# A two-layer hybrid decoder trunk: the memory's keys scaled for both token tiles together, and two pieces of side work moved by units

## The chip, the cores and the metric

The kernel runs on one core of one Trainium2 chip. The time is the device time of an execution in microseconds; the time of a kernel is the median of its runs. Three runs of the kernel before gave 929.42 us in the median, from 928.89 to 930.27.

## The reference

Two layers, sequence of 256, width 1024, batch 1, all in float32. Each layer normalises x and multiplies it with one combined matrix `w_in`, whose columns feed four branches and their gates:

```python
h = rmsnorm(x, norm_mix[l])
z = h @ w_in[l]
z_gm, z_lru, q_s, k_s, v_s, q_x, z_gate = jnp.split(z, IN_SPLITS, axis=-1)
mem_n = rmsnorm(mem, norm_mem[l])
o = [gmlp(z_gm), rglru(z_lru), swa(q_s, k_s, v_s), cross(q_x, mem_n)]
x = x + jnp.sum(sigmoid(z_gate + b_gate) * (o @ w_branch), axis=2) @ w_out[l]
x = x + jnp.square(jax.nn.relu(rmsnorm(x) @ w_ff1[l])) @ w_ff2[l]
```

Two branches matter here. Cross attention has 4 heads of 128 and looks at 256 tokens of a memory: `k, v = split(mem_n @ w_kv)`, keys and queries normalised per head, softmax over the 256 tokens. The RG-LRU branch convolves over 4 positions, then multiplies the result with two block-diagonal matrices, whose sigmoids are its gates, and runs a linear recurrence.

## The kernel before, in words

Tokens lie in two tiles of 128 ("token tile 0 and 1"). Weights come in chunks of 128x1024 floats, called units. For each unit, SP's queue loads the raw chunk (L178), ACT copies it to a rounded format (`wh`, L201) and DVE subtracts that from the raw values (`wl`, L202). `prep` (L182) does this some units ahead, as far as raw tiles (4) and weight tiles (5 pairs) come free. TensorE then multiplies with `wh` and `wl` (all through L255), so that a product in full precision is three matmuls. A unit of a 512-column projection is 12 matmuls of 512 columns.

Results land in PSUM, in two pools of four banks: `ps_mm` (tiles `mm`) for the projections, `ps_ac` (tiles `ac`) for transposes, attention and gates. At the start of a layer TensorE computes, in this order: the memory's keys (units 0 to 3, two `mm` banks, one for each token tile of the memory), the memory's values (units 4 to 7, the other two), the input of the RG-LRU branch (`proj_cols`, L413, units 8 to 11; in the first layer its first half goes to `ac` banks and its second half, units 10 and 11, to `mm` banks), cross attention's queries (12 to 15), the window attention's queries (16 to 19), its keys and values (20 and 21), the gMLP (22 to 29), the RG-LRU's second input (30 to 33), and the branch gates.

What isn't a projection is written as generators in a list, `side`. After each unit (after each two in `proj_cols`), `tick` tops up the weights and calls `next` once on each generator. A bare `yield` therefore means "not before the next unit". An instruction that goes through `late` (L362) is, in the first layer, pinned behind everything traced before it on its engine, which is how a yield sets its earliest place on TensorE. `after(ins, ref)` (L354) pins one instruction behind another one in the order of the same engine, without a wait. Within these pins a planner orders each engine's instructions by simulated times, and the engines then run their queues in that order.

`mem_k_side` (L442) takes the keys' two `mm` banks. For each token tile m it sums squares per head on ACT (`head_sq`, L426 and L431: four squares, each with the read of an accumulator), forms a mean on DVE (L449) and the power -1/2 on POOL (L377), multiplies it with the memory's own norm `rmem` on DVE (L452), and scales the four heads on ACT into SBUF (L455). Only this last step frees the `mm` bank. `rmem` and `rmem2` come from `mem_norm` (L1156 to L1163). `st["scaled", m]` names the last scaling of tile m; the split of unit 11 is pinned behind that of tile 0, the splits of units 12 to 14 and the evacuation of the values (L473) behind that of tile 1. Behind eight yields the keys are transposed (L466).

`xa_side` (L523) copies the queries (L530), sums squares, and one unit later transposes them (L542, L543); another unit later it starts `xa_tok` (L552) for token tile 0 and two units behind that for tile 1. Each computes its scores in two `ac` banks, a softmax (exponentials at L501), transposes of the probabilities (L518, L520) and products with the values.

`lru_side` (L716) convolves on DVE (L727, L730), waits some units, and then computes the gates (two matmuls with `wbd` for each of two column blocks, sigmoids at L740 and L741).

Of the kernel before, what the change touches and what calls it, by code (L numbers as in the profile page):

```python
# [13 lines left out]
AF = mybir.ActivationFunctionType  # L14
ALU = mybir.AluOpType
AX = mybir.AxisListType

P = 128
# [6 lines left out]
EPS = 1e-6  # L25
# [16 lines left out]
def trunk(ctx, tc, x_d, mem_d, memT_d, pc_d, pr_d, bg_d, cs_d, wsT_d, wr_d, wi_d,  # L42
          w_in, w_mem_kv, w_branch, w_out, w_ff1, w_ff2, out_d):
    nc = tc.nc
    act, dve, pool, pe = nc.scalar, nc.vector, nc.gpsimd, nc.tensor
# [23 lines left out]
    def T(pl, shape, dt, tag):  # L69
        cnt[0] += 1  # L70
        return pl.tile(shape, dt, tag=tag, name=f"{tag}_{cnt[0]}")
# [4 lines left out]
    def tq():  # L76
        return T(tqp, [P, 512], F32, "tq")

    def a4():
        return T(a4p, [P, 4, S], F32, "a4")  # L80
# [7 lines left out]
    def pac():  # L88
        return T(ps_ac, [P, 512], F32, "ac")

    def small(n):
        return T(sm, [P, n], F32, f"s{n}")
# [161 lines left out]
    def mm(out, lhsT, rhs, start, stop):  # L254
        return pe.matmul(out, lhsT=lhsT, rhs=rhs, start=start, stop=stop, skip_group_check=True)  # L255
# [18 lines left out]
    def join(out, ps, ref=None):  # L274

        after(act.activation(out=out, in_=ps[:, 1, :], func=AF.Copy), ref)
        dve.tensor_tensor(out=out, in0=ps[:, 0, :], in1=out, op=ALU.add)
# [8 lines left out]
    rmem = T(const, [P, 2], F32, "rmem")  # L286
    rmem2 = T(const, [P, 2], F32, "rmem2")
# [61 lines left out]
    def rsqrt_small(ss, n, inv):  # L349
        ms = small(n)  # L350
        dve.tensor_scalar(out=ms, in0=ss, scalar1=inv, scalar2=EPS, op0=ALU.mult, op1=ALU.add)
        return pow_half(ms, n)

    def after(ins, ref):  # L354

        if ref is not None:
            tc.add_manual_dep(ins.ins, ref.ins.name,
                              mybir.DependencyInfo(mybir.DependencyClass.NoSync, mybir.DependencyReason.DATA),
                              reason="after")
        return ins  # L360

    def late(l, ins):  # L362

        return tc.keep_in_program_order(ins) if l == 0 else ins
# [10 lines left out]
    def pow_half(ms, n):  # L375
        r = small(n)
        pool.tensor_tensor(out=r, in0=ms, in1=mhalf[:, 0:n], op=ALU.pow)  # L377
        return r
# [44 lines left out]

    st = {}

    def head_sq(src, nh, hd, ref):  # L426

        ss = small(nh)
        for h in range(nh):
            junk = tq()[:, 0:hd]  # L430
            after(act.activation(out=junk, in_=src[:, h * hd:(h + 1) * hd], func=AF.Square, accum_out=ss[:, h:h + 1]),  # L431
                  ref)
        return ss
# [8 lines left out]
    def mem_k_side(l, kT, ps):  # L442
        while st["hs"] in side:
            yield
        ks = []
        for m in range(2):
            ss = head_sq(ps[m], 4, P, st["square"] if l or m else st["split", 7])
            ms = small(4)
            dve.tensor_scalar(out=ms, in0=ss, scalar1=rmem2[:, m:m + 1], scalar2=EPS, op0=ALU.mult, op1=ALU.add)  # L449
            r = pow_half(ms, 4)  # L450
            rk = small(4)
            dve.tensor_scalar(out=rk, in0=r, scalar1=rmem[:, m:m + 1], scalar2=0.0, op0=ALU.mult, op1=ALU.add)  # L452
            k = tq()
            for h in range(4):
                st["scaled", m] = act.activation(out=k[:, h * P:(h + 1) * P], in_=ps[m][:, h * P:(h + 1) * P],  # L455
                                                 func=AF.Copy, scale=rk[:, h:h + 1])
            ks.append(k)
        yield
        while st["hs"] in side:
            yield  # L460
        for _ in range(6 if l else 8):
            yield
        for m in range(2):
            pst = pac().rearrange("p (h t) -> p h t", t=P)
            for h in range(4):
                late(l, pe.transpose(pst[:, h, :], ks[m][:, h * P:(h + 1) * P], ident))  # L466
            act.activation(out=kT[:, :, m * P:(m + 1) * P], in_=pst, func=AF.Copy,
                           scale=pc[l][:, C_XK:C_XK + 1])
# [54 lines left out]
    def xa_side(l, ps):  # L523

        oh, ol = st["o"][3]
        qT = a4()
        qs, rs = [], []
        for t in range(2):
            q = tq()
            act.activation(out=q, in_=ps[t], func=AF.Copy)  # L530
            qs.append(q)
        for t in range(2):
            ss = head_sq(ps[t], 4, P, None)
            r = rsqrt_small(ss, 4, 1.0 / P)
            rsc = T(odd, [P, 4], F32, f"xrs{t}")
            dve.tensor_scalar(out=rsc, in0=r, scalar1=P ** -0.5, scalar2=0.0, op0=ALU.mult, op1=ALU.add)
            rs.append(rsc)
        yield
        for t in range(2):
            pst = pac().rearrange("p (h t) -> p h t", t=P)  # L540
            for h in range(4):
                pe.transpose(pst[:, h, :], qs[t][:, h * P:(h + 1) * P], ident)  # L542
            act.activation(out=qT[:, :, t * P:(t + 1) * P], in_=pst, func=AF.Copy,  # L543
                           scale=pc[l][:, C_XQ:C_XQ + 1])
        yield
        kT = st["kTx"]
        for t in range(2):
            side.append(xa_tok(l, t, qT, kT, rs[t], oh, ol))
            yield
            yield  # L550
# [162 lines left out]
    def l2():  # L713
        return T(l2p, [P, 2, S], F32, "l2")

    def lru_side(l, ps, c0):  # L716


        pcl = pc[l]
        xc, r, ig, sq = l2(), l2(), l2(), l2()  # L720
        for j in range(2):
            c = c0 + j
            xb = T(t1p, [P, S + 4], F32, "t1")
            pool.memset(xb[:, 0:3], 0.0)
            join(xb[:, 3:S + 3], ps[j], None if l else st["values"])
            w = [pcl[:, C_CW + 4 * k + c:C_CW + 4 * k + c + 1] for k in range(4)]
            dve.tensor_scalar(out=xc[:, j, :], in0=xb[:, 0:S], scalar1=w[0], scalar2=pcl[:, C_CB + c:C_CB + c + 1],  # L727
                              op0=ALU.mult, op1=ALU.add)
            for k in range(1, 4):
                dve.scalar_tensor_tensor(out=xc[:, j, :], in0=xb[:, k:k + S], scalar=w[k], in1=xc[:, j, :],  # L730
                                         op0=ALU.mult, op1=ALU.add)
        for _ in range((3 if c0 == 0 else 1) + (0 if l else 3)):

            yield
        for j in range(2):
            c = c0 + j
            pg = pac().rearrange("p (a s) -> p a s", a=2)
            for i in range(2):
                late(l, mm(pg[:, i, :], wbd[i][:, c, :], xc[:, j, :], True, True))
            act.activation(out=r[:, j, :], in_=pg[:, 0, :], func=AF.Sigmoid, bias=pcl[:, C_BR + c:C_BR + c + 1])  # L740
            st["sigmoid"] = act.activation(out=ig[:, j, :], in_=pg[:, 1, :], func=AF.Sigmoid,  # L741
                                           bias=pcl[:, C_BI + c:C_BI + c + 1])
        dve.tensor_tensor(out=ig, in0=ig, in1=xc, op=ALU.mult)
        yield
        for j in range(2):
            c = c0 + j
            after(act.activation(out=xc[:, j, :], in_=r[:, j, :], func=AF.Exp, scale=nsp8[l][:, c:c + 1]),
                  st["sigmoid"])
            act.activation(out=r[:, j, :], in_=r[:, j, :], func=AF.Tanh, scale=nsp4[l][:, c:c + 1])
        yield  # L750
        while "sqrt" not in st:
            yield
        tc.keep_in_program_order(act.activation(out=sq, in_=r, func=AF.Sqrt, scale=-1.0))
        dve.scalar_tensor_tensor(out=r, in0=xc, scalar=1.0, in1=r, op0=ALU.add, op1=ALU.mult)
        dve.tensor_scalar(out=r, in0=r, scalar1=1.0, scalar2=0.0, op0=ALU.add, op1=ALU.add)
        dve.scalar_tensor_tensor(out=sq, in0=xc, scalar=1.0, in1=sq, op0=ALU.add, op1=ALU.mult)
        dve.tensor_tensor(out=ig, in0=ig, in1=sq, op=ALU.mult)
        for j in range(2):
            dve.tensor_tensor_scan(out=xc[:, j, :], data0=r[:, j, :], data1=ig[:, j, :], initial=0.0,
                                   op0=ALU.mult, op1=ALU.add)  # L760
        yield
        while "gb" not in st:
            yield
        oh, ol = st["o"][1]
        for j in range(2):
            c = c0 + j
            o = t1()
            dve.tensor_tensor(out=o, in0=xc[:, j, :], in1=st["gb"][:, c, :], op=ALU.mult)
            split(o, oh[:, c, :], ol[:, c, :])
# [397 lines left out]
    for l in range(DEPTH):  # L1167
        st["h"] = new_h()
        h, lo = halves(st["h"])
# [58 lines left out]
```

## Time and profile before

| | |
|---|---|
| median of three runs | 929.42 us |
| profiled execution | 930.37 us |
| its span, first to last instruction | 928.6 us |
| TensorE busy (matmuls) | 922.4 us, 99% |
| VectorE (DVE) busy | 642.2 us, 69% |
| ScalarE (ACT) busy | 545.5 us, 59% |
| GpSimd (POOL) busy | 47.5 us, 5% |
| bytes moved by DMA | 173.56 MB, 187 GB/s in the mean |

Busy times are unions of an engine's instructions. Matmuls overlap each other in the record, so a row's duration is a little longer than the distance to the next row's start. "Idle before" is the time an engine had nothing running ahead of an instruction, with the instruction that released it. The granted clock is a share of TensorE's full 2.4 GHz.

### The profile page before, as it was taken

Reading aid. Unit: us, or ns where it says so; the run is one execution under the profiler, and the core shown is the slowest. Engines: PE = TensorE matmul, PEld = TensorE weight load, DVE = VectorE, ACT = ScalarE, POOL = GpSimd, SP = SyncE. Lnnn points to the kernel's source line nnn. Section 1 sums busy time; section 2 is a strip of 40 time slices with the busy share of each in tenths; the row PEclk is TensorE's granted clock in tenths of the full one; section 3 lists DMA queues with packets and bytes.
Section 4 is the critical chain, followed back from the end, with each engine's and each line's share of the span. In section 5 each row is a group of like instructions: output and inputs, shape, how many; then the busy total and the mean of one; then the engine's idle time right before and its main releaser. Section 6 shows DMA issues by size and latency. Waiting matters only on the chain.

```text
span 928.6 us, 12959 instructions
## 1 busy us (share of the span) xinstructions
PE 922.4 (99%) x4712; PEld 777.4 (84%) x4712; DVE 642.2 (69%) x1055; ACT 545.5 (59%) x913; POOL 47.5 (5%) x93
## 2 busy tenths in 40 slices
PE   9999999999999999999999999999999999999998
PEld 6788887888889888888888888888888898888887
DVE  6686878656686766776577587865666767666663
ACT  7778898444444744645376788874444455544541
POOL 1114300000000000000010230000000000000000
PEclk9999999999999999999999999999999999999999
DMA  9683445666565776776456444466665657666641
GB/s 342 193 253 113 140 153 178 201 216 209 188 196 148 234 228 184 231 234 187 149 163 197 147 133 153 142 185 213 203 213 177 195 175 233 199 190 195 199 141 46
DMA packets 143920, 173.56 MB, mean 187 GB/s; under 512 B 8176, under 2 KB 92656, under 8 KB 143856
## 3 DMA queue, kind: packets, MB, share of 16 engines
q1 hardware_dynamic: 143424, 172.31, 59.9%
q8 instruction: 37, 0.61, 0.3%
q10 hardware_dynamic: 432, 0.43, 0.2%
q14 instruction: 27, 0.22, 0.1%
HBM read 171.66 MB, written 1.05 MB: 186 GB/s over the span
## 4 chain that ended last, share of the span: by engine, by line
PE 95%; DMA 1%; ACT 1%; DVE 1%; issue 1%; POOL 0%; SPq 0%; ACTq 0%
PE mm L255 65%; PE ac L255 28%; DMA raw<-in_w_mem_kv 1%; PE ac L518 1%; DVE wl L202 0%; ACT wh L201 0%; PE mm L801 0%; PE mm L972 0%; POOL s L377 0%; ACT hx L806 0%; PE ac L709 0%; ACT tq L455 0%; ACT tq L431 0%; PE ac L801 0%; PE ac L466 0%
## 5 line engine op out<-in xcount | busy, mean ns | idle before, releaser
L202 DVE TENSOR_TENSOR wl<-raw,wh 128x1024 fp32r<-128x1024 f32 (+1 forms) x276 | 332.3, 1209 | 176.3 <-ACT wh L201 175.9
L201 ACT ACTIVATE wh<-raw 128x1024 fp32r<-128x1024 f32 (+1 forms) x276 | 287.6, 1048 | 254.0 <-PE mm L255 137.3
L255 PE MATMUL mm<-wh,hx 128*128 128x512 f32 (+1 forms) x832 | 257.5, 387 | 0.0
L255 PEld LDWEIGHTS mm<-wh,hx 128*128 128x128 f32 x832 | 153.4, 188 | 29.8 <-issue 0.8
L255 PE MATMUL mm<-wl,hx 128*128 128x512 f32 (+1 forms) x416 | 160.1, 385 | 0.0
L255 PE MATMUL mm<-hx,wh 128*128 128x512 f32 (+1 forms) x496 | 122.4, 381 | 1.8 <-ACT tq L455 1.8
L255 PE MATMUL ac<-wh,s 128*128 128x512 f32 x380 | 121.5, 390 | 0.0
L255 PEld LDWEIGHTS mm<-hx,wh 128*128 128x128 f32 x496 | 89.9, 190 | 17.5 <-ACT tq L455 2.0
L255 PEld LDWEIGHTS mm<-wl,hx 128*128 128x128 f32 x416 | 78.3, 188 | 15.0 <-issue 0.3
L255 PEld LDWEIGHTS ac<-wh,s 128*128 128x128 f32 x380 | 71.4, 188 | 14.4
L255 PE MATMUL ac<-wl,s 128*128 128x512 f32 x190 | 74.2, 390 | 0.0
L255 PE MATMUL mm<-hx,wl 128*128 128x256 f32 x464 | 69.9, 283 | 0.0
L255 PEld LDWEIGHTS mm<-hx,wl 128*128 128x128 f32 x464 | 65.5, 191 | 4.7 <-issue 0.3
L202 DVE TENSOR_TENSOR a<-raw,a 128x1024 fp32r<-128x1024 f32 x32 | 39.2, 1225 | 27.4 <-ACT a L201 27.4
L201 ACT ACTIVATE a<-raw 128x1024 fp32r<-128x1024 f32 x32 | 33.9, 1059 | 38.7 <-PE ac L255 21.5
L255 PE MATMUL mm<-wl,o0h 128*128 128x512 f32 x128 | 50.3, 393 | 0.0
L255 PE MATMUL mm<-wh,o0l 128*128 128x512 f32 x128 | 49.8, 389 | 0.0
L255 PE MATMUL mm<-wh,o0h 128*128 128x512 f32 x128 | 48.7, 395 | 0.0
L255 PE MATMUL mm<-hx,a 128*128 128x512 f32 (+1 forms) x256 | 46.4, 336 | 0.0
L255 PE MATMUL ac<-a,s 128*128 128x512 f32 x192 | 45.7, 390 | 0.0
L255 PEld LDWEIGHTS mm<-hx,a 128*128 128x128 f32 x256 | 40.7, 189 | 5.8
L255 PEld LDWEIGHTS ac<-a,s 128*128 128x128 f32 x192 | 35.5, 188 | 7.1
(214 smaller groups left out, 1146.5 us busy)
## 6 DMA issues: line engine op xcount, KB each, us to landing
raw<-in_w_ff SPq DMA_DIRECT2D x128, 512.0 KB, 4.3
raw<-in_w_in SPq DMA_DIRECT2D x116, 512.0 KB, 4.0
raw<-in_w_branch SPq DMA_DIRECT2D x32, 512.0 KB, 3.6
raw<-in_w_out SPq DMA_DIRECT2D x16, 512.0 KB, 3.6
raw<-in_w_mem_kv SPq DMA_DIRECT2D x12, 512.0 KB, 3.5
bg<-in_bg SPq DMA_DIRECT2D x16, 256.0 KB, 4.0
raw<-in_w_mem_kv SPq DMA_DIRECT2D x8, 256.0 KB, 5.6
xt<-in_x SPq DMA_DIRECT2D x2, 512.0 KB, 6.5
```

Of the source, the lines that this page charges most:

```text
L201: a1 = act.activation(out=wh[:, sl, :], in_=v[:, sl, :], func=AF.Copy)
L202: a2 = dve.tensor_tensor(out=wl[:, sl, :], in0=v[:, sl, :], in1=wh[:, sl, :].bitcast(F32), op=ALU.subtract)
L255: return pe.matmul(out, lhsT=lhsT, rhs=rhs, start=start, stop=stop, skip_group_check=True)
L518: late(l, pe.transpose(ps[:, h, :], Pt[:, h, kt * P:(kt + 1) * P], ident))
```

## The change

In the first layer, `mem_k_side` treats both token tiles in one pass: the squares of both go into one small tile of 8 columns, two means, one power over 8 columns, two factors, and then the eight scalings. The squares of tile 1 are pinned behind the last split of h (`st["turned"][0]`) in place of the memory's own squares. In the second layer the loop still runs tile by tile. `xa_side` yields four times instead of once ahead of the scores in the first layer, and `lru_side` four times instead of three (beside its 3 or 1) ahead of the gates.

```diff
-    def head_sq(src, nh, hd, ref):
-        ss = small(nh)
+    def head_sq(src, nh, hd, ref=None, ss=None):
+        ss = small(nh) if ss is None else ss
...
-        for m in range(2):
-            ss = head_sq(ps[m], 4, P, st["square"] if l or m else st["split", 7])
-            ms = small(4)
-            dve.tensor_scalar(out=ms, in0=ss, scalar1=rmem2[:, m:m + 1], ...)
-            r = pow_half(ms, 4)
-            rk = small(4)
-            dve.tensor_scalar(out=rk, in0=r, scalar1=rmem[:, m:m + 1], ...)
-            k = tq()
-            for h in range(4):
-                st["scaled", m] = act.activation(out=k[:, h * P:(h + 1) * P], ...)
-            ks.append(k)
+        for ms_ in ((0,), (1,)) if l else ((0, 1),):
+            n = 4 * len(ms_)
+            ss, ms, rk = small(n), small(n), small(n)
+            for i, m in enumerate(ms_):
+                head_sq(ps[m], 4, P, st["square"] if l else st["turned"][0] if m else st["split", 7],
+                        ss[:, 4 * i:4 * i + 4])
+            for i, m in enumerate(ms_):
+                h4 = slice(4 * i, 4 * i + 4)
+                dve.tensor_scalar(out=ms[:, h4], in0=ss[:, h4], scalar1=rmem2[:, m:m + 1], ...)
+            r = pow_half(ms, n)
+            for i, m in enumerate(ms_):
+                h4 = slice(4 * i, 4 * i + 4)
+                dve.tensor_scalar(out=rk[:, h4], in0=r[:, h4], scalar1=rmem[:, m:m + 1], ...)
+            for i, m in enumerate(ms_):
+                k = tq()
+                for h in range(4):
+                    st["scaled", m] = act.activation(out=k[:, h * P:(h + 1) * P], ...)
+                ks.append(k)
...
-        yield
+        for _ in range(1 if l else 4):
+            yield
         kT = st["kTx"]
...
-        for _ in range((3 if c0 == 0 else 1) + (0 if l else 3)):
+        for _ in range((3 if c0 == 0 else 1) + (0 if l else 4)):
```

## Rows read from the trace of the kernel before

**Rows 1.** The page: busy time of TensorE, and the costliest group of ACT
```profile
PE 922.4 (99%) x4712; PEld 777.4 (84%) x4712; DVE 642.2 (69%) x1055; ACT 545.5 (59%) x913; POOL 47.5 (5%) x93
...
L201 ACT ACTIVATE wh<-raw 128x1024 fp32r<-128x1024 f32 (+1 forms) x276 | 287.6, 1048 | 254.0 <-PE mm L255 137.3
```
**Rows 2.** Waits of TensorE: line, waited for, us in total, times, longest
```profile
PE mm L255 <- ACT tq L455: 1.8, 1, 1.8
PE ac L255 <- DVE t L1121: 1.3, 1, 1.3
```
**Rows 3.** Busy time by stretch, behind the wait; clock, DMA share, GB/s last
```profile
40.80:44.50 3.70, 3.70 (x10) 2.95 (x11) 1.63 (x2) 3.70 (x7) 0.00 (x0) 0.54 0.15 35
44.50:47.00 2.50, 2.50 (x16) 2.20 (x15) 2.50 (x5) 2.28 (x4) 0.00 (x0) 1.00 0.69 209
```
**Rows 4.** Timeline of TensorE, 36 to 46: start, us, what, idle before
```profile
36.02 2.00 PE L255 MATMUL mm<-hx,wh 128*128 128x512 f32 x8
37.86 1.11 PE L255 MATMUL mm<-hx,wl 128*128 128x256 f32 x8
40.79 3.56 PE L255 MATMUL mm<-hx,wh 128*128 128x512 f32 x8 [1.82 <-ACT tq L455]
...
45.26 0.63 PE L255 MATMUL mm<-wh,hx 128*128 128x512 f32 x2
```
**Rows 5.** Chain of work that ended last, 20 to 60: start, us, what
```profile
21.42 1.03 ACT tq L431 x8
```
**Rows 6.** Timeline of DVE, ACT and POOL, 29 to 43, and the power of 8
```profile
29.62 0.15 DVE L1163 SCALAR_TENSOR_TENSOR rmem<-s 128x2 f32<-128x2 f32 x1
31.20 1.94 POOL L377 TENSOR_TENSOR s<-s,mhalf 128x4 f32<-128x4 f32 x1 [1.54 <-DVE s L449]
33.81 1.15 ACT L455 ACTIVATE tq<-mm,s 128x128 f32<-128x128 f32 x4 [1.23 <-DVE t L332]
35.58 1.10 ACT L201 ACTIVATE wh<-raw 128x1024 fp32r<-128x1024 f32 x1
38.23 1.01 POOL L377 TENSOR_TENSOR s<-s,mhalf 128x4 f32<-128x4 f32 x1 [5.09 <-DVE t L339]
39.59 1.15 ACT L455 ACTIVATE tq<-mm,s 128x128 f32<-128x128 f32 x4 [2.66 <-DVE t L341]
40.61 1.28 ACT L473 ACTIVATE a<-mm,rmem 128x512 f32<-128x512 f32 x2
41.75 2.04 ACT L201 ACTIVATE wh<-raw 128x1024 fp32r<-128x1024 f32 x2
42.87 1.23 DVE L202 TENSOR_TENSOR wl<-raw,wh 128x1024 fp32r<-128x1024 f32 x1 [2.91 <-ACT wh L201]
...
79.16 1.65 POOL L377 TENSOR_TENSOR s<-s,mhalf 128x8 f32<-128x8 f32 x1 [0.62 <-DVE s L351]
```
**Rows 7.** Timeline, 60 to 179: convolution, gates, scores, softmax, products, branch projections
```profile
60.60 0.48 DVE L730 SCALAR_TENSOR_TENSOR l<-t,pc,l 128x256 f32<-128x256 f32 x1
64.32 1.28 ACT L740 ACT_TABLE_LOAD   x1
64.34 1.89 PE L255 MATMUL ac<-l,wbd 128*128 128x256 f32 x8
65.61 0.47 ACT L740 ACTIVATE l<-ac,pc 128x256 f32<-128x256 f32 x1
73.74 1.25 ACT L543 ACTIVATE a<-ac,pc 128x512 f32<-128x512 f32 x2
75.47 3.62 PE L255 MATMUL ac<-a,a 128*128 128x256 f32 x16
89.43 0.57 ACT L501 ACTIVATE s<-ac,s,xrs 128x256 f32<-128x256 f32 x1
101.05 1.09 ACT L520 ACTIVATE pt<-ac 128x512 f32<-128x512 f32 x2
102.68 1.95 PE L255 MATMUL ac<-pt,a 128*128 128x128 f32 x16
178.26 0.39 PE L255 MATMUL mm<-wh,o1h 128*128 128x512 f32 x1
```

More of the change, by code (lines that the diff above doesn't have):

```diff
@@ L445, in mem_k_side @@
         ks = []
-        for m in range(2):
-            ss = head_sq(ps[m], 4, P, st["square"] if l or m else st["split", 7])
-            ms = small(4)
-            dve.tensor_scalar(out=ms, in0=ss, scalar1=rmem2[:, m:m + 1], scalar2=EPS, op0=ALU.mult, op1=ALU.add)
-            r = pow_half(ms, 4)
-            rk = small(4)
-            dve.tensor_scalar(out=rk, in0=r, scalar1=rmem[:, m:m + 1], scalar2=0.0, op0=ALU.mult, op1=ALU.add)
-            k = tq()
-            for h in range(4):
-                st["scaled", m] = act.activation(out=k[:, h * P:(h + 1) * P], in_=ps[m][:, h * P:(h + 1) * P],
-                                                 func=AF.Copy, scale=rk[:, h:h + 1])
-            ks.append(k)
+        for ms_ in ((0,), (1,)) if l else ((0, 1),):
[6 more added lines that the diff above has]
+                h4 = slice(4 * i, 4 * i + 4)
+                dve.tensor_scalar(out=ms[:, h4], in0=ss[:, h4], scalar1=rmem2[:, m:m + 1], scalar2=EPS,
+                                  op0=ALU.mult, op1=ALU.add)
+            r = pow_half(ms, n)
+            for i, m in enumerate(ms_):
+                h4 = slice(4 * i, 4 * i + 4)
+                dve.tensor_scalar(out=rk[:, h4], in0=r[:, h4], scalar1=rmem[:, m:m + 1], scalar2=0.0,
+                                  op0=ALU.mult, op1=ALU.add)
+            for i, m in enumerate(ms_):
+                k = tq()
+                for h in range(4):
+                    st["scaled", m] = act.activation(out=k[:, h * P:(h + 1) * P], in_=ps[m][:, h * P:(h + 1) * P],
+                                                     func=AF.Copy, scale=rk[:, 4 * i + h:4 * i + h + 1])
+                ks.append(k)
         yield
@@ L532, in xa_side @@
         for t in range(2):
-            ss = head_sq(ps[t], 4, P, None)
+            ss = head_sq(ps[t], 4, P)
             r = rsqrt_small(ss, 4, 1.0 / P)
```

## The prediction

> **What bounds the kernel now.** I read the page's first part, the list of waits for TensorE, the stretches around its one long wait, and then the timeline of the other engines back from it. TensorE is busy for 922.4 of 928.6 us [rows 1], so a change of this kind can only take away what TensorE waits, or add to it. The waits name one place inside the layers: 1.8 us, once, for ACT's scaling of the memory's keys at L455 [rows 2]. The clock falls behind it: in the 3.70 us that follow, the granted clock is 0.54 in the mean, and 1.00 again in the next stretch [rows 3]. The matmuls say the same: eight of 512 columns take 2.00 us ahead of the wait and 3.56 us behind it [rows 4]; that is the lower of the two levels, 1.2 instead of 2.4 GHz. So the place costs 1.82 + 3.70 x (1 - 0.54) = 1.82 + 1.70 = 3.52 us.
>
> Why it waits is seen one step back. The second half of the convolution's projection takes two banks of `ps_mm`. The first comes free with the scaling of token tile 0, the second with that of tile 1. Tile 0 is through at 33.81 + 1.15 = 34.96 [rows 6], before TensorE asks at 36.02 [rows 4]. Tile 1 starts its squares only behind tile 0's scaling, and its mean, power and factor follow: power at 38.23, scaling from 39.59 to 40.74 [rows 6]. TensorE could have gone on at 40.79 - 1.82 = 38.97.
>
> **The keys in one go.** ACT: the four squares of tile 1 (with their reads eight instructions; those of tile 0 took 1.03 us [rows 5]) move from behind tile 0's scaling to anywhere behind the last split of h. Nothing is added there. DVE: two means and two factors remain. POOL: two powers of 4 columns (1.94 and 1.01 us) become one of 8. The trace has that form later, at 1.65 us. The first power of 4 was 0.93 us dearer than the second, so I bound the new one by 1.65 and 1.65 + 0.93 = 2.58 us, and take 1.65, the row of its own form [rows 6].
>
> The chain's times: the means can follow rmem2, through at 29.62 + 0.15 = 29.77; before, the power began at 31.20. ACT idles for 1.23 us ahead of 33.81, so the squares find room; if they stand in front instead, the power begins 1.03 us later. So it begins between 31.2 and 32.2, and ends at 32.9 (or 34.8). One factor and the handover took 33.81 - (31.20 + 1.94) = 0.67 us, so I put 0.9 for two: 33.8 (or 35.7). Four scalings take 1.15 us, eight 2.3. Tile 0 is through at 34.9 (or 36.8), tile 1 at 36.1 (or 38.0). If the split of weights for TensorE's next unit (1.10 us at 35.58, pinned behind tile 0's scaling) is put between the two, tile 1 is at 39.1 in the worst case. Needed: 36.02 and 38.97. What is left of the wait lies between nothing and 0.8 us; I take 0.1, from the near end of both. It can't fall below nothing, as TensorE waits nowhere else near it. At the other end, if the order on ACT undoes the edit, all 3.52 us stay.
>
> **What is late next.** With 3.4 us off, the next unit (cross attention's queries, 45.26 before) starts at about 41.9. Its two banks come free with the evacuation of the values (1.28 us, behind the scaling), so at 37.4 to 40.4. Its weights need a split on ACT and a difference on DVE. Before, the difference began 42.87 - 40.74 = 2.1 us behind the scaling and took 1.2. Behind a scaling that ends at 36.1 to 38.0, with 1.1 us for the unit before it, it is through at 40.5 to 42.4; it is wanted two matmuls behind the unit's start, at 42.3. Covered, with nothing to spare at the worse end. The raw tiles' transfers follow these differences in SP's queue, so they come earlier too; the DMA engines are busy for a share of 0.15 behind the wait [rows 3], so there is room. Farther on the splits run ahead: of the 254.0 us that ACT idles in front of them, 137.3 are waits for TensorE to give tiles back [rows 1].
>
> **Gates one unit later.** The gates' matmuls keep their number and size. Before, the convolution's last step ends at 60.60 + 0.48 = 61.08 and the gates start at 64.34 [rows 7]: 3.3 us to spare, and TensorE now comes 3.4 us earlier. Of 512 columns, eight matmuls start within 37.86 - 36.02 = 1.84 us, so a unit of 12 is 2.8 us, and the pin one unit later keeps 3.3 - 3.4 + 2.8 = 2.7 us even if DVE were no earlier. Cost: nothing. Without this edit it would be 0.1 us at most.
>
> **Scores three units later.** The queries' transposed copy ends at 73.74 + 1.25 = 74.99 and the scores begin at 75.47 [rows 7]: 0.5 us to spare. 3.4 us earlier, TensorE would stand here for up to 2.9 us. Three units are 8.3 us, which leaves 8.3 + 0.5 - 3.4 = 5.4 us to spare. Both tokens' scores ran as one block of 16; now the second is pinned two units behind the first, and softmax, transposes and products with the values go along. The result is wanted when TensorE turns to the branch projections at 178.26 [rows 7], 70 us and more behind. Cost: nothing. In exchange the softmax moves in among square roots and GELUs on ACT. A load of an activation table took 1.28 us, and the activation behind it began 0.01 us later (64.32 to 65.61 [rows 7]). Two more (there and back) would be 2.6 us of ACT.
> The Trainium skill ("ScalarE: Activation LUTs", What ACT_TABLE_LOAD costs) puts a switch at about 2.66 us, drain included, so by it those two would be 5.3 us; the row shows no drain behind the load, and the row decides. The same page (Table sets: the hidden batching unit) advises to finish one set's functions before the next, which speaks against this move.
>
> **Sum.** 930.37 us is the profiled execution (span 928.6 and 1.8 around it). 930.37 - 3.52 + 0.1 = 926.95. It ran 0.95 above the median of 929.42, so for the median: 929.42 - 3.42 = 926.0 us. Layer 1 keeps its numbers and its order of work, as both loops have the old form there.
>
> **Rivals.**
> *Given back farther on.* The products with the values start 0.5 us after the copy they need (101.05 + 1.09 = 102.14 against 102.68 [rows 7]). If at such a place ACT and DVE, which carry the same work as before, don't move along, TensorE waits 3.4 - 0.5 = 2.9 us and a gain of 0.5 stays: 928.9. With half of it given back: 927.5. Two more table loads in that chain would do it as well. For it: the slack is that small. Against: the place at 38.97 held up ACT too (2.66 us idle before 39.59 [rows 6]), so ACT and DVE start earlier as well, and cross attention leaves this stretch.
> *It doesn't do what it says.* The order on ACT (split, evacuation or squares ahead of tile 1's scaling) keeps tile 1 well beyond 38.97 and the clock falls again: 929.4. Against: even the worst bound above is 39.1.
> *Slower.* The scores hold two of four `ps_ac` banks per token until their exponentials have read them. Before, the second token's were held from 75.47 + 3.62 = 79.09 to 89.43 + 0.57 = 90.00 [rows 7], 10.9 us. Three units later that hold stands where the window attention's transposes ask for banks. If TensorE stands for half of it, 5.5 us, and loses the clock for 1.70 us once more, the sum is 929.42 - 3.42 + 7.2 = 933.2. It decides from 3.4 + 1.9 = 5.3 us of new waits on. Against: before, both tokens held all four banks at once, and no wait of TensorE on one is listed [rows 2].
>
> **How the numbers follow.** Forecast 0.68; given back 0.17, half of that in part and half in whole; not done 0.06; slower 0.09. A measurement of this kernel tells about 0.2% from no change, which is 1.9 us. Faster by more: 0.68 + 0.08 = 0.76. Within: 0.08 + 0.06 = 0.14. Slower: 0.10 with rounding. The low end is all 3.52 us off and the 0.8 us by which the runs before lie apart around their median, 925.1. The high end takes in the gain given back and some of the runs' spread, 929.1; the slower case and most of the undone one lie outside.
>
> **What would show it.** Right: no wait of TensorE at L455, a granted clock of 1.00 from 20 us on, one power of 8 columns near 31 to 35 us, tile 1 scaled by 38, the queries' projection starting near 42, and everything behind it 3.4 us earlier. Wrong: a wait of TensorE on an `ac` bank or a copy between 70 and 110 us, a second stretch at the lower clock, or table loads in a softmax with TensorE waiting behind it.

## The result: 934.33 us, slower by about half a per cent, and the profile after

The changed kernel took 934.33 us in the median of six executions (933.50 to 935.92); the kernel before took 929.28 us beside it (six executions). The ratio is 1.0054 (95% interval [1.0043, 1.0064]), so it is slower, by 5.0 us, where the forecast was 926.0 us and its range ended at 929.1 us. The profiled execution took 934.35 us with a span of 932.6 us, against 930.37 and 928.6.

In the new listing the lines have moved: the scaling of the keys is L465 (was L455), the evacuation of the values L483 (L473), exponentials L511 (L501), the exponential of the window attention's sink L516, normalising L521 (L511), transposes of the probabilities L528 (L518) and their copy L530 (L520). L653 (L642) transposes the window attention's keys and L655 (L644) copies them out of their `ac` bank into `kk`. L912 (L901) is a GELU of the gMLP, L697 (L686) its squares, L931 (L920) the GELU of the RG-LRU's second input (`gb`), L764 (L753) a square root of the RG-LRU.

First the edit itself. The timelines of POOL and ACT after show it (start, us, what, idle before):

```profile
30.56 1.64 POOL L377 TENSOR_TENSOR s<-s,mhalf 128x8 f32<-128x8 f32 x1 [0.74 <-DVE s L455]
...
33.36 2.18 ACT L465 ACTIVATE tq<-mm,s 128x128 f32<-128x128 f32 x8
35.38 1.32 ACT L483 ACTIVATE a<-mm,rmem 128x512 f32<-128x512 f32 x2
```

One power of 8 columns takes 1.64 us, and both tiles are scaled at 33.36 + 2.18 = 35.54, where tile 1 was through at 40.74 before [rows 6]. The waits of TensorE after no longer name that place, but two others (line, waited for, us in total, times, longest):

```profile
PE ac L528 <- DVE s L521: 2.4, 1, 2.4
PE ac L528 <- ACT kk L655: 1.4, 1, 1.4
PE ac L255 <- DVE t L1132: 1.3, 1, 1.3
```

The third row is the one of the kernel's start that stood there before [rows 2]. The stretches of the profile after, with TensorE's granted clock in the third column from the end, show the same:

```profile
36.00:45.00 9.00, 9.00 (x49) 7.73 (x48) 8.15 (x21) 6.75 (x11) 0.00 (x0) 1.00 0.69 215
...
128.90:132.30 3.40, 3.11 (x10) 2.54 (x11) 3.40 (x10) 2.51 (x5) 0.00 (x0) 0.53 0.68 222
133.00:140.00 7.00, 7.00 (x40) 5.23 (x40) 6.41 (x15) 6.48 (x14) 0.00 (x0) 1.00 0.46 149
```

Around the old wait TensorE is now busy for all of 9.00 us at full clock. The half clock hasn't gone, though: it has moved behind the longer of the new waits, where it costs 3.40 x (1 - 0.53) = 1.60 us in this execution. (Of the six, one has a granted clock of 1.00 over the span, at 933.50 us, the others 0.997 or 0.998.) TensorE's timeline after puts both into the run of things:

```profile
35.70 2.00 PE L255 MATMUL mm<-hx,wh 128*128 128x512 f32 x8
...
41.74 0.40 PE L255 MATMUL mm<-wl,hx 128*128 128x512 f32 x1
...
100.64 0.66 PE L528 MATMUL ac<-ident,s 128*128 128x128 f32 x4 [1.40 <-ACT kk L655]
...
129.19 0.88 PE L528 MATMUL ac<-ident,s 128*128 128x128 f32 x3 [2.36 <-DVE s L521]
...
182.24 0.39 PE L255 MATMUL mm<-wh,o1h 128*128 128x512 f32 x1
```

Three of these rows are marks to measure by. From unit 10's first matmul to the first `wl` matmul of cross attention's queries (unit 12), the distance was 45.73 - 36.02 = 9.71 us in the profile of before (the matmul at 45.73 follows the row at 45.26 in [rows 4]), and is 41.74 - 35.70 = 6.04 us now: 3.67 us gained. From there to the first matmul of the branch projections it was 178.26 - 45.73 = 132.53 us [rows 7] and is 182.24 - 41.74 = 140.50 us: 7.97 us lost. Of those, 1.40 + 2.36 are the waits and 1.60 the half clock. The other 2.6 us are hardly idle time: between the two marks TensorE is idle for 3.85 us, 0.09 more than the two waits, where before it wasn't idle at all, and it is busy for 136.65 us in place of 132.53. So beside the half clock some 2.5 us lie in rows of matmuls that follow each other more slowly. From 182 us to the end nothing differs: the lag at that matmul, 3.98 us, is that of the span, 4.0.

**Why the shorter wait.** ACT's timeline ahead of it, after:

```profile
95.44 1.28 ACT L912 ACT_TABLE_LOAD   x1
96.73 1.08 ACT L912 ACTIVATE tq<-mm 128x512 f32<-128x512 f32 x2
97.70 1.06 ACT L201 ACTIVATE wh<-raw 128x1024 fp32r<-128x1024 f32 x1
98.65 0.63 ACT L697 ACTIVATE tq<-tq 128x512 f32<-128x512 f32 x1
...
99.27 1.05 ACT L201 ACTIVATE wh<-raw 128x1024 fp32r<-128x1024 f32 x1
100.21 0.65 ACT L655 ACTIVATE kk<-ac 128x256 f32<-128x256 f32 x2
```

ACT isn't idle for a moment here. The `kk` copies, which free an `ac` bank, stand last in the queue behind a table load, two GELUs, a square and two splits, 100.21 - 95.44 = 4.77 us in all.

That queue on ACT isn't new. Before, the copies stood still farther behind the same GELUs, whose table load came at 96.75. New is TensorE's order. The first two rows are TensorE's and ACT's of before, the third is TensorE's of after:

```profile
104.47 0.60 PE L642 MATMUL ac<-ident,t 128*128 128x128 f32 x4
105.16 0.66 ACT L644 ACTIVATE kk<-ac 128x256 f32<-128x256 f32 x2
...
94.80 0.38 PE L653 MATMUL ac<-ident,t 128*128 128x128 f32 x2
```

Before, the keys' transposes followed the products of cross attention's second token (102.68 [rows 7]), and their copies came 0.7 us later. With the scores moved, the transposes come ahead of both tokens' products, from 94.80 on, and their banks are held until ACT gets to the copies, 5.4 us later. The runs below bear this out: the transposes come behind both tokens' products in the three that leave the scores where they were (97.28 with the keys alone), and ahead of them in the five that move them.

**Why the longer one.** The same engine 25 us later, after:

```profile
122.12 0.48 ACT L511 ACTIVATE s<-s,s,srs 128x128 f32<-128x128 f32 x1
...
123.20 1.28 ACT L931 ACT_TABLE_LOAD   x1
124.49 0.63 ACT L931 ACTIVATE gb<-gb 128x512 f32<-128x512 f32 x1
125.14 1.28 ACT L516 ACT_TABLE_LOAD   x1
126.44 0.21 ACT L516 ACTIVATE s<-s 128x4 f32<-128x4 f32 x1
126.55 1.04 ACT L201 ACTIVATE wh<-raw 128x1024 fp32r<-128x1024 f32 x1
```

A GELU and its two table loads stand in the middle of a softmax of the window attention, between the last of its four exponentials and the small one of its sink: 126.44 - 123.20 = 3.24 us. Before, ACT went from the load for a softmax's exponentials to its sink without a load between (timeline before):

```profile
123.87 1.28 ACT L501 ACT_TABLE_LOAD   x1
...
127.96 0.19 ACT L506 ACTIVATE s<-s 128x4 f32<-128x4 f32 x1
...
128.44 1.28 ACT L920 ACT_TABLE_LOAD   x1
```

DVE then adds to it (timeline after):

```profile
126.67 0.16 DVE L517 TENSOR_TENSOR s<-s,s 128x4 f32<-128x4 f32 x1 [0.76 <-ACT s L516]
126.87 0.18 DVE L519 RECIPROCAL s<-s 128x4 f32<-128x4 f32 x1
127.62 1.23 DVE L202 TENSOR_TENSOR wl<-raw,wh 128x1024 fp32r<-128x1024 f32 x1 [0.57 <-ACT wh L201]
128.76 0.87 DVE L521 TENSOR_SCALAR s<-s,s 128x128 f32<-128x128 f32 x4
```

The softmax's sum is complete at 126.83 and its reciprocal at 127.05, but a weight difference, which itself waits 0.57 us for its split on ACT, goes ahead of the normalising that TensorE waits for. That begins at 128.76, so by this trace DVE's order accounts for some 1.7 of the 2.36 us; ACT's order is what let it come to that, as the pin below shows. The page's first part sums it up for ACT: 550.8 us busy in 916 instructions, before 545.5 in 913 [rows 1]. Three more table loads (29 against 26 in the two traces) are 3 x 1.28 = 3.8 of the 5.3 us:

```profile
PE 924.3 (99%) x4712; PEld 777.9 (83%) x4712; DVE 642.5 (69%) x1055; ACT 550.8 (59%) x916; POOL 46.0 (5%) x92
```

### The profile page after: what moved, and what is told of

It reads as the page before. It is cut to its first block, busy times and chain, and to the rows that moved or that the text cites. A ratio compares the mean times of both kernels' runs of the same rounds, so it can differ in the third digit from the quotient of the medians.

```text
span 932.6 us, 12960 instructions
## 1 busy us (share of the span) xinstructions
PE 924.3 (99%) x4712; PEld 777.9 (83%) x4712; DVE 642.5 (69%) x1055; ACT 550.8 (59%) x916; POOL 46.0 (5%) x92
## 4 chain that ended last, share of the span: by engine, by line
PE 89%; ACT 4%; DMA 2%; issue 2%; DVE 2%; POOL 1%; SPq 0%; ACTq 0%; POOLq 0%; DVEq 0%
PE mm L255 59%; PE ac L255 27%; ACT wh L201 1%; DMA raw<-in_w_mem_kv 1%; DVE wl L202 1%; PE ac L528 1%; DMA raw<-in_w_in 1%; PE mm L812 0%; PE mm L983 0%; ACT s L511 0%; ACT hx L817 0%; POOL s L377 0%; ACT L511 0%; DVE l L741 0%; SPq L303 0%
## 5 line engine op out<-in xcount | busy, mean ns | idle before, releaser
L201 ACT ACTIVATE wh<-raw 128x1024 fp32r<-128x1024 f32 (+1 forms) x276 | 288.0, 1050 | 257.3 <-PE mm L255 140.4
L201 ACT ACTIVATE a<-raw 128x1024 fp32r<-128x1024 f32 x32 | 33.9, 1060 | 37.8 <-PE ac L255 21.3
```

The lines of the kernel that those rows point to most:

```text
L201: a1 = act.activation(out=wh[:, sl, :], in_=v[:, sl, :], func=AF.Copy)
```

## The experiments

Four theories were put to the test. A: each loss comes from an instruction that the planner put into a bad place in ACT's queue, and pinning it elsewhere takes the loss away. B: the move of the scores makes the loss, and the keys alone would gain. C: TensorE now comes too early for ACT and DVE whatever their order, so that a gain of some 3 us can't be kept. D (formed after the first runs): the half clock behind the old wait belongs to some executions only, and so most of the 1.70 us that the forecast counted for it weren't there to be gained.

**Keys in one go, without the two moves.**

```diff
-        for _ in range(1 if l else 4):
+        for _ in range(1):
             yield
         kT = st["kTx"]
...
-        for _ in range((3 if c0 == 0 else 1) + (0 if l else 4)):
+        for _ in range((3 if c0 == 0 else 1) + (0 if l else 3)):
```

> Only the keys in one go; gates and scores at their old yields. Theory A (each part costs by what it does to ACT's order): the wait at the keys' scaling is gone, worth 4.0 us by the start of the window attention's queries, and 2.4 us of wait and 1.7 us of half clock come back, because ACT's queue here too has a GELU and two table loads inside a softmax of the window attention: 928 to 931 us. Theory B (the scores' move alone makes the loss): nothing comes back, 925 to 926 us. Theory C (TensorE comes too early for ACT and DVE, whatever the order): waits spread over many places behind 75 us, 933 us and more.

Measured: 928.68 us (928.27 to 929.55, 11 executions), ratio 0.9992 [0.9983, 1.0001], span 926.7. So even the keys alone can't be told from no change. The waits of TensorE in this kernel, beside the one of the start:

```profile
PE ac L528 <- DVE s L521: 0.8, 1, 0.8
PE ac L255 <- DVE s L498: 0.3, 1, 0.3
```

and ACT's timeline ahead of the first of them (the exponentials end at 119.97):

```profile
121.78 1.28 ACT L931 ACT_TABLE_LOAD   x1
123.07 0.63 ACT L931 ACTIVATE gb<-gb 128x512 f32<-128x512 f32 x1
123.72 1.28 ACT L516 ACT_TABLE_LOAD   x1
```

The GELU splits the softmax here too, at a lower price. So that placing comes already with the keys alone, and theory B can't be the whole. Nor does TensorE stand at cross attention's scores, which the forecast moved to spare it a wait there: they begin at 68.98 and 72.98 us, and the copies that they need are through at 66.28 + 0.67 = 66.95 and 69.80 + 0.67 = 70.47.

**The two moves, with the old keys.** The kernel before with this edit alone:

```diff
-        yield
+        for _ in range(1 if l else 4):
+            yield
         kT = st["kTx"]
...
-        for _ in range((3 if c0 == 0 else 1) + (0 if l else 3)):
+        for _ in range((3 if c0 == 0 else 1) + (0 if l else 4)):
```

> Only the moves: gates one unit and scores three units later, the keys as before. Theory A: the wait of 1.8 us at the keys stays, with its half clock; ACT's queue has the exponentials of the second token behind the square root, and the GELU inside the window's softmax, so TensorE waits for the window keys' copies (about 1.4 us) and for the softmax (about 2.4 us, and 1.7 us of clock): 933 to 938 us. Theory B: the same or up to 938. Theory C: without an early TensorE there is nothing to lose, 929 to 930 us.

Measured: 937.63 us (936.50 to 939.40, 4 executions), ratio 1.0089 [1.0075, 1.0102]. Its waits hold the old one and both new ones, at nearly the size that they have in the changed kernel (line numbers are those of before):

```profile
PE ac L518 <- DVE s L511: 2.4, 1, 2.4
PE mm L255 <- ACT tq L455: 1.5, 1, 1.5
PE ac L518 <- ACT kk L645: 1.3, 1, 1.3
```

The moves by themselves cost 937.63 - 928.95 = 8.7 us, and on top of the keys 934.33 - 928.68 = 5.6 us. No TensorE that is early is needed for them, which speaks against C.

**The gates' unit taken back.** The changed kernel, with the second line of the first diff alone (`(0 if l else 3)` ahead of the gates).

> The changed kernel with the gates at their old yield. The instructions stand in the same order on every engine as in the changed kernel, so the gates' unit does nothing: 933.5 to 935 us, the time of the changed kernel. Rival (the gates' unit has a share in the loss or in the gain): outside 933 to 936 us.

Measured: 935.01 us (933.58 to 935.37, 5 executions), ratio 1.0052 [1.0039, 1.0064], with the same waits:

```profile
PE ac L528 <- DVE s L521: 2.9, 2, 2.4
PE ac L528 <- ACT kk L655: 1.4, 1, 1.4
```

The traces of the two kernels have the same order of instructions on every engine, so the gates' unit does nothing, and on the new keys the moves' cost is the scores' alone. (Keys and gates without the scores weren't run.) In this execution the wait at 129 us is 2.36 us long as well, and the granted clock behind it is 1.00 from 129 to 133 us.

**The GELU pinned behind the softmax.** The changed kernel, with the GELU of `gb` after the sink's exponential in ACT's order. A pin of this kind is no wait.

```diff
-            act.activation(out=e, in_=e, func=AF.Exp)
+            st["sink"] = act.activation(out=e, in_=e, func=AF.Exp)
...
-                act.activation(out=gb[:, c:c + 2, :], in_=gb[:, c:c + 2, :], func=AF.Gelu_apprx_tanh)
+                after(act.activation(out=gb[:, c:c + 2, :], in_=gb[:, c:c + 2, :], func=AF.Gelu_apprx_tanh), st["sink"])
```

> The changed kernel with one pin on ACT: the GELU of the RG-LRU's second input stands behind the sink's exponential of the last window softmax traced before it, so no table load falls inside a softmax. Theory A: the wait of 2.4 us at 126 us and the second half-clock stretch go, 4.1 us and some small pieces: 929 to 930.5 us, with the 1.4 us wait for the window keys' copies still there. Theory B and C: the wait moves to another place, 933 us or more.

Measured: 932.07 us (930.67 to 933.04, 11 executions), ratio 1.0023 [1.0014, 1.0033]. The softmax's wait is gone, and the other stays:

```profile
PE ac L528 <- ACT kk L655: 1.4, 1, 1.4
```

That is 2.3 us of the loss, less than was expected. In the profiled execution, of 933.04 us, the half clock now follows the `kk` wait (0.55 in the mean from 102.70 to 106.20). Of the eleven executions four have a granted clock of 0.998 (932.39 to 933.04), and seven 1.00 (930.67 to 932.62). (A further wait, of 1.3 us for L201, lies at 6 us; some executions of other kernels have one there too.)

**Both pinned.** The same, and the GELU of L912 behind the copy of `kk`:

```diff
-            act.activation(out=kk[:, :, tsl], in_=pst, func=AF.Copy)
+            st["kk"] = act.activation(out=kk[:, :, tsl], in_=pst, func=AF.Copy)
...
-                act.activation(out=v, in_=ps[n], func=AF.Gelu_apprx_tanh)
+                after(act.activation(out=v, in_=ps[n], func=AF.Gelu_apprx_tanh), st["kk"])
```

> As the kernel with the GELU pin, and the GELU of the gMLP's gated half stands behind the copies of the window attention's keys on ACT. Theory A: both waits go and the gain at the keys stays: 926 to 928.5 us. Theory B and C: 931 us or more, as TensorE finds other waits.

Measured: 928.62 us (928.25 to 929.23, 11 executions), ratio 0.9992 [0.9983, 1.0001]. Both waits are gone; beside the one of the start there is one row left. ACT's timeline shows the new order, the copy ahead of the table load:

```profile
PE ac L631 <- POOL tq L597: 0.2, 1, 0.2
```

```profile
97.44 0.68 ACT L655 ACTIVATE kk<-ac 128x256 f32<-128x256 f32 x2
98.13 1.28 ACT L912 ACT_TABLE_LOAD   x1
```

All executions have a granted clock of 0.999 or 1.00. Two pins, which take no operation away, give 934.33 - 928.62 = 5.7 us back. (The new order needs two table loads fewer, 27 in place of 29.) This is theory A for the two waits and for the clock behind them. It still misses what A expected, by 0.1 us, and isn't the forecast's gain.

**Only the second pin.** The changed kernel with the `kk` pin alone, to see what each does without the other.

> The changed kernel with the pin of the gMLP's GELU behind the window keys' copies alone. With it the planner puts the sink's exponential ahead of the RG-LRU's GELU by itself, so neither wait should be there. Theory A: 928 to 929.5 us, as with both pins. Rival (the second pin does work of its own): 931 us or more.

Measured: 930.12 us (929.79 to 931.67, 11 executions), ratio 1.0007 [0.9998, 1.0016]. A miss by 0.6 us. With this pin the planner puts the sink's exponential ahead of the GELU by itself, so the wait at 129 goes as well, but another comes at the next window softmax:

```profile
PE ac L528 <- DVE s L521: 1.5, 1, 1.5
```

One pin changes what the planner does 25 us farther on. So the pins' effects don't add up, and the difference between two kernels that differ in one pin isn't that pin's price.

**Keys alone, with the GELU pin, and with both.** The first diff (no moves) together with the fourth, and with the fourth and fifth.

> Only the keys in one go (gates and scores at their old yields), and the GELU pin. Theory A with D: the 0.8 us wait that the split softmax costs there goes, so against the kernel before 1.8 us of wait and some 0.3 us less are left: 926.8 to 928 us. Rival (the planner's order gives it back elsewhere): 928.5 us or more.

> As the one before, and the window keys' copies ahead of the gMLP's GELU. Theory A with D: no wait in TensorE's list but the warm-up's, 926.5 to 928 us. Rival: 928.5 us or more.

Measured: 927.86 us (927.43 to 929.09, 11 executions), ratio 0.9981 [0.9972, 0.9990], with the GELU pin; 927.55 us (927.14 to 929.34, 11 executions), ratio 0.9981 [0.9972, 0.9989], with both. These beat the kernel before by about 0.2%, and the changed one by more. TensorE is as early in the second of them as in the changed kernel, and waits nowhere but at the start; the waits and the timeline's two marks are:

```profile
PE ac L255 <- DVE t L1132: 1.3, 1, 1.3
```

```profile
41.70 0.40 PE L255 MATMUL mm<-wl,hx 128*128 128x512 f32 x1
...
175.02 0.39 PE L255 MATMUL mm<-wh,o1h 128*128 128x512 f32 x1
```

Between the marks lie 133.32 us, 0.8 more than before, where the changed kernel has 140.50. This refutes C: ACT and DVE carry a TensorE that comes this early, if their order is right. It also shows what the scores' move costs when both pins are in: 928.62 - 927.55 = 1.1 us, with 0.2 us of listed wait. So the pins take away most of its cost and not all of it.

**The kernel before, profiled again.** Three single executions, for theory D: what does the clock do behind the old wait in other executions?

> The kernel before once more, one look. In its 27 timed executions the granted clock over the span is 0.999 to 1.000 in 21, at a median near 928.9 us, and 0.998 in 6, at 930.25 us and more; the profiled one was of the second kind. Theory D (the half clock behind the keys' wait is an event of some executions): most likely 928.8 to 929.2 us, with the wait of 1.8 us at the keys and a granted clock of 1.00 behind it. Rival (the half clock belongs to the wait): 0.998, the stretch of 3.4 us at half clock is there again.

> The kernel before, one look. Of 48 timed executions 34 had a granted clock of 0.999 or 1.000 over the span (median 928.9 us) and 14 had 0.998 (median 930.4 us). Theory D (the half clock behind the wait of 1.8 us comes in some executions only): in a look of the first kind the wait is listed, the clock behind it is 1.00, and the time is 928.7 to 929.2 us. Rival (the two kinds differ in something else than this place): the half clock stands behind the wait in a fast look too.

> The kernel before, a further look, for the same question: 928.7 to 929.2 us without a half clock behind the wait, or 930.3 us and more with it; the rival is a time that doesn't go with the clock.

Measured: 930.79 us with a granted clock of 0.998 over the span, 932.08 us with 0.998, and 928.76 us with 1.00. In the first two TensorE waits for 1.86 and 2.73 us and the half clock follows (0.55 from 42.70 to 46.20 and from 42.80 to 46.00), as in the profile that the forecast read; so far the rival had it right. In the third (timeline of TensorE, and stretches):

```profile
35.38 2.00 PE L255 MATMUL mm<-hx,wh 128*128 128x512 f32 x8
...
40.63 2.12 PE L255 MATMUL mm<-hx,wh 128*128 128x512 f32 x8 [2.29 <-ACT tq L455]
...
44.00 0.49 PE L255 MATMUL mm<-wl,hx 128*128 128x512 f32 x1
```

```profile
40.00:44.00 4.00, 3.37 (x19) 2.76 (x19) 1.29 (x2) 4.00 (x9) 0.00 (x0) 1.00 0.35 112
44.00:48.00 4.00, 4.00 (x19) 3.31 (x19) 4.00 (x8) 2.65 (x6) 0.00 (x0) 1.00 0.70 171
```

The wait is 2.29 us and the clock stays at 1.00. Of the 63 executions of the kernel before that ran beside the experiments, 43 have a granted clock of 0.999 or more (median 928.95 us, 928.60 to 930.03), and 20 have 0.998 (median 930.36 us, 929.97 to 932.33). They lie 1.4 us apart. The profile on which the forecast rested, at 930.37 us, is one of the second kind, and the median is one of the first. Theory D holds as far as four profiles of this kernel show: the half clock stands behind the wait in the three at 0.998 and not in the one at 1.00. That the 20 lost their time at this same place is argued from the 1.4 us, and wasn't profiled.

## Why the prediction was wrong, step by step

**The keys in one go: right.** No wait at the scaling; the power 1.64 us (taken: 1.65), begun at 30.56 (31.2 to 32.2, so somewhat earlier than reckoned), both tiles scaled at 35.54 (36.1). The place gave 3.67 us against the 3.42 predicted, in the profile of that kind.

**The term of 1.70 us for the clock: right for its execution, wrong for the median.** The forecast took the whole 3.42 us off a median whose executions mostly have no half clock there. Against the execution at 1.00 the same distance (first matmul of unit 10 to the first `wl` matmul of the queries) is 44.00 - 35.38 = 8.62 us before and 6.04 after, a gain of 2.58 us. With every later loss but 0.8 us pinned away, a ratio of 0.9981 is left, 1.8 us. With 2.58 in place of 3.42 us the forecast would have been 929.42 - 2.58 = 926.8 us, still inside its range: this step made the gain smaller and not a loss.

**Scores three units later, "Cost: nothing": the step that failed.** It counted TensorE's slack at the scores (5.4 us) and the 70 us until the result is wanted, and took the two more table loads as 2.6 us of ACT's time. ACT has the time: it is busy for 59% of the span. What it doesn't have is the order. The softmax's exponentials came to stand among GELUs and a square root; TensorE transposed the window attention's keys ahead of the products, while the `kk` copies that free their banks stood 4.77 us deep in ACT's queue; and a GELU stood inside the window attention's softmax, which it does with the keys alone too, for a wait of 0.8 us. TensorE waited 1.40 and 2.36 us behind them and ran 3.40 us at 0.53. The cost of this step is 5.6 us on the new keys and 8.7 us on the old ones (the runs with and without the moves). Nor was the wait of up to 2.9 us there that the move was to spare: with the keys alone, the scores at their old yield start 2.0 and 2.5 us behind their copies.

**The rivals.** The second half of *Given back farther on*, two more table loads in a chain that TensorE waits for, names this mechanism, for cross attention's chain; it struck in the window attention's instead. Its price was too low, 2.9 us at most, as it reckoned with one place and with the full clock behind it. The rival on the slower side had the size (933.2 us) but not the cause. The wait on an `ac` bank is there at 100.64, yet what holds the bank is a late copy of `kk` and not scores, and a GELU pinned behind that copy in ACT's order takes the wait away. All three signs of being wrong that the forecast named are in the profile: the wait on a bank, a second stretch at the lower clock, and table loads in a softmax.

A load of 1.28 us and an activation 0.02 us behind it (125.14 to 126.44) stand in the trace again, so the two loads and the GELU between them took 3.24 us. With 2.66 us for a switch, as the Trainium skill ("ScalarE: Activation LUTs", What ACT_TABLE_LOAD costs) has it, they would have taken 2 x 2.66 + 0.63 = 6.0 us, an estimate from its figure. The Trainium skill's advice to finish one set's functions before the next (the same page, Table sets: the hidden batching unit) was the warning that bore on this change, and the prediction quoted it and then set the cost to nothing.

**What is late next, gates, second layer: right.** The queries' units run without a listed wait. The gates' unit does nothing. Behind 182 us nothing differs.

**Open.** Of the 7.97 us, 2.6 us are neither a listed wait nor the half clock, and nearly all of that is busy time of TensorE. The keys alone lose 134.65 - 132.53 = 2.1 us over that stretch with 1.1 us of listed waits (its marks are at 41.66 and 176.31), and 0.8 us remain with both pins and no waits; here too the rest is busy time. Which matmuls it lies in was not settled, nor why the moves cost 3.1 us more on the old keys than on the new ones. Nor was it tried to find a place for the scores between one and four units.

## What to carry to other kernels

An engine that is busy for 59% of the time can still be the one that decides, by the order of its queue: before a piece of side work is moved, look at what stands around its new place on each in-order engine, above all at table sets and at copies that free a bank. Where a planner orders the queues, ask what it will do with every other instruction of that stretch. If a gain is lost, test each part of the change alone, and look for two or three instructions to pin: here taking the scores' move back gave as much (928.68 us) as two pins with the move kept (928.62), and both together gave most (927.55). Take the size of a gain from several executions: a profile shows one of them, and a stretch at half clock may belong to that one alone.

## What the runs showed of the hardware that had not been expected

The granted clock behind a wait of TensorE isn't settled by the wait's length. A wait of 1.82 us was followed by 3.70 us at 0.54 in the mean [rows 3], one of 1.86 us by a half clock in another execution, and one of 2.29 us, at the same place of the same kernel, by none. The changed kernel and the one with the gates' unit taken back run the same order on every engine; behind the same wait of 2.36 us the clock was 0.53 in the one execution and 1.00 in the other. Of 63 executions of the kernel before, 20 have a mean clock of 0.998.
